# Rows of 1 / rms by a diagonal and a product with ones in place of a store and a load

## The chip, the core and the metric

The kernel runs on one core of a Trainium2 chip. The core has five engines, each with an instruction queue of its own that it works through in order: TensorE (PE in the profile; the load of its weights is shown apart as PEld), VectorE (DVE), ScalarE (ACT), GpSimd (POOL) and SyncE (SP), which in this kernel issues nearly all of the DMAs. Engines meet by semaphores. TensorE reads its operands from SBUF and writes to PSUM, which is cut into banks of 128 partitions by 512 float32 numbers. SBUF and PSUM have 128 partitions; an engine that works by elements works within each partition, so a value that lies along the partitions has to be moved before it can be used along the free axis.

The metric is the device time of one execution, in microseconds (us); lower is better.

## The reference, cut to what matters

One layer of an encoder, on x of 2048 tokens by 1024 channels in float32, with a memory of 256 tokens:

```python
xn = rmsnorm(h, norm_mix_g)
proj = xn @ w_in                      # columns: q, k, v (512 each), u, y (512 each)
q, k = rope(q, positions), rope(k, positions)
attn = dilated_mixture_attention(q, k, v)      # 8 heads of 64, three windows
uc = centred_depthwise_conv(u, conv_w, conv_b)
rec = bidirectional_rglru(uc, ...) * gelu(y)   # gates, two scans over the tokens
h = h + concatenate([attn, rec]) @ w_out
h = h + memory_cross_attention(rmsnorm(h, norm_cross_g), rmsnorm(mem, norm_mem_g),
                               w_cq, w_ck, w_cv, w_co)   # 4 heads of 128
hid = square(relu(rmsnorm(h, norm_mlp_g) @ w_mlp_in))    # 4096 channels
h = h + hid @ w_mlp_out
return rmsnorm(h, norm_final_g)

def rmsnorm(x, g):
    return x * rsqrt(mean(x * x, axis=-1) + 1e-6) * g
```

So there are five norms: of x, of the memory, and of h three times. Each needs one number 1 / rms for every token.

## The kernel before, in words

**Layout.** Activations are kept with channels on the partitions and tokens on the free axis: a tile is 128 channels by 512 tokens. A norm sums over channels, so over the partitions, and its factor 1 / rms differs from token to token, so along the free axis. To multiply a tile by it, the factors of 512 tokens have to lie in every one of the 128 partitions: a **row** tile of 128 x 512, all partitions alike. Since the factor of a token can be taken out of a product over channels, the products run on the values without the norm, and the row is multiplied onto the result as it leaves PSUM. The gain g goes into the operands.

**Products in three parts.** Every large product is `mm3` (L120 to L123): both operands are split into a high and a low part in float32r, and three matmuls (high by high, high by low, low by high) add up in one PSUM bank. That is why L121, L122 and L123 come three at a time in the profile. PSUM banks are given out by tag: `ps("mm")` takes turns between m0 and m1, `ps("mmb")` between m0, m1 and b; each tag has two banks in the phases that matter here (b has two, a has two). Most instructions have tile names, which the profile shows: `xh`, `xl` are the parts of x, `wh`, `wl` those of weights, `mh`, `ml` of the memory.

**How a row is made (`RowSum`, L125 to L173).** `add` squares a tile on ACT (L142) and adds it to `ss` on POOL or DVE (L144). `columns` (L147 to L156) sums `ss` over the partitions: for each 128 tokens one matmul of `ss` by a column of ones (L151), into a bank of tag a, so that the sums of 128 tokens lie along the partitions, one column for each 128. DVE copies these columns out (L155), and POOL makes 1 / rms of them in two instructions (`rstd_of`, L116 to L118). From the columns the row is then made in one of two ways:

- `rows` (L158 to L161): SP stores the columns to a line in DRAM, 4 bytes apiece (L160), and loads the line back into all 128 partitions (L161). SP issues the load only after the store has landed.
- `rows_now` (L163 to L173): DVE multiplies the identity by the columns into `dg`, four diagonal 128 x 128 blocks beside each other (L167); PE multiplies a 128 x 128 tile of ones by it in float32, which puts into every partition the one entry of each column (L172), in a bank of tag b; ACT copies the bank into the row (L173). The tile of ones is allocated and set by POOL each time (L171).

**Where rows are made.** Fifteen rows go by `rows`, five by `rows_now`:

- *The memory*, one row `rbm` of 256 tokens, in `memory_kv` (L294), after the first of eight column blocks of the keys and values; L296 multiplies it onto `em`.
- *x*, four rows `rbn` of 512 tokens, two for each half B of the tokens, in `row_tables` (L349 to L353), called by `uy_unit` after the second product of the first unit in each 512 tokens; L416 multiplies them onto `e`, and `fill_tables` multiplies them into the tables of rope. Only the columns of all 16 blocks of 128 tokens stay (`rsb`). The first half of the tokens comes round once more later (for v, k and q), and `tables` loads its row again from the same line (L344).
- *v*, two rows `svr` of 256 numbers, in `v_unit` (L455). They do not come from activations but from the columns of the v weights: 1 / rms of each column, used to bring v to a size that fits float16 (L458), and taken out again later by `dsc`.
- *h after the first residual*, four rows `rb1`, in `half_out` (L911 to L955): the sums of block b are made while block b + 1 runs, `columns` ahead of its tile 4 and `rows` ahead of its tile 5; those of the last block stand behind its last tile. Used in `query` (L1003 to L1014).
- *h after the second residual*, four rows `rb2`, in the loop of the cross attention (L1235 and L1246) and, the last, at the start of the MLP (L1391). Used by `t_raws` (L1099 on).
- *h after the third residual*, five rows by `rows_now` in `close` (L1425): they are the last thing before the output is written, 512 or 256 tokens each.

**What sets the order.** The code is written in Tile, a framework that allocates tiles, sets the semaphores and plans the order of each engine's queue from priorities (mostly the order of the code) and its own estimates of durations; the order that comes out can differ from that of the text. In the first stage, `block` (L582 on) runs over units of the combined projection: u and y of the first half of the tokens, the memory, u and y of the second half, then v, k and q of both halves. From the second half on, the steps of the RG-LRU (`lru`, L470 on: convolution, gates, scans) are a generator that `pace` advances by 1.3 steps for each part of a unit, so that DVE, ACT and POOL do the RG-LRU while PE does the projection. The convolution loads `u` back from DRAM (L492); its gates take banks of tag a (L518 on) and two small `mm3` each.

Then the attention of the eight heads, the output projection (`half_out`), the cross attention with the output of block b - 1 woven into block b, and the MLP in two large stages.

**Names that the change touches**, beside those above: the DRAM lines `rs_d`, `rsm_d`, `sv_d`, `r1_d`, `r2_d` (L60 to L64); `small` (constants); `vs`, the `RowSum` for v (L595), whose tiles are taken from the rings `rl` and `rh` of the rope; the `RowSum` of `Cross.co` (L1067), whose tiles for the fourth block lie in other pools; and `ss` and `sq`, the tiles of a `RowSum`.

## Time and profile before

| | |
|---|---|
| time, median of 3 runs | 2923.38 us (2919.47 to 2930.01) |
| the profiled execution's own time | 2928.47 us |
| its span, first instruction to last | 2926.6 us |
| mean granted TensorE clock | 0.942 |
| rows that go by store and load | 15 |
| rows that go by diagonal and product | 5 |

The page gives the span in 40 equal slices; with 2926.6 us a slice is 73.2 us. Each digit is the busy share in tenths, PEclk the granted TensorE clock in tenths of full speed, DMA the mean busy share of the core's 16 DMA engines.

```profile
PE   7897776776779989897997899989999999999997
DVE  6644656765678878634567754474447999999997
ACT  5527355461646656623444233343333333334342
POOL 2222120203334434343124655555655776666652
PEclk9998888888789999898998999999999999999999
DMA  7452334426667876554344433343336222122213
```

Slices 1 to 10 are the combined projection with the RG-LRU beside it, 11 to 16 the attention, 17 and 18 the output projection, 19 to 22 the cross attention, and from there on the MLP with the final norm. In the queues of DMA nearly all of the packets belong to SP's issues (q1); POOL issues a few itself (q0).

```profile
q1 hardware_dynamic: 262864, 342.19, 38.3%
q0 software_dynamic: 4288, 27.27, 4.0%
```

Columns: packets, MB, share of the 16 engines' span. In the rows of groups, an instruction stands with its line, engine, operation, output and input tiles, count, then busy time in all and mean ns of one, then the idle time of that engine just before them and what ended most of it. In the rows of a timeline, the first number is the start in us from the start of the span, the second the duration, and the bracket holds the idle time before and the instruction that ended it.

### The profile page before, as it was taken

The numbers are of one execution on the slowest core, as the hardware profiler recorded it, in microseconds if no ns is written. First come the engines' busy times: TensorE is split into PE (matmuls) and PEld (weight loads), VectorE is DVE, ScalarE is ACT, GpSimd is POOL, SyncE is SP. The second block draws the span as 40 slices with busy tenths as digits, with TensorE's granted clock in tenths as the row PEclk, the third lists the DMA queues.
The fourth block names the chain that finished last, engine by engine and source line by source line (L and its number), as shares of the span: only waits on it lengthen the run. The fifth ranks groups of instructions, "written<-read, shape, count | busy, mean of one in ns | idle before, by whom it ended". The sixth has DMA issues, their size and how long they took to land. (4 is left out here: it accounts for less than half of the span.)

```text
span 2926.6 us, 39992 instructions
## 1 busy us (share of the span) xinstructions
PE 2590.2 (89%) x14074; PEld 2196.7 (75%) x14074; DVE 2010.9 (69%) x3361; ACT 1277.1 (44%) x2349; POOL 1256.2 (43%) x888
## 2 busy tenths in 40 slices
PE   7897776776779989897997899989999999999997
PEld 6776665665679989786885788868887777778776
DVE  6644656765678878634567754474447999999997
ACT  5527355461646656623444233343333333334342
POOL 2222120203334434343124655555655776666652
PEclk9998888888789999898998999999999999999999
DMA  7452334426667876554344433343336222122213
GB/s 194 144 133 82 105 81 145 123 96 156 180 170 189 216 181 155 187 160 123 101 136 142 143 109 112 109 140 112 112 108 216 86 73 87 65 87 80 72 58 115
DMA packets 267352, 372.00 MB, mean 127 GB/s; under 512 B 93072, under 2 KB 139792, under 8 KB 264080
## 3 DMA queue, kind: packets, MB, share of 16 engines
q1 hardware_dynamic: 262864, 342.19, 38.3%
q0 software_dynamic: 4288, 27.27, 4.0%
q8 instruction: 111, 1.82, 0.3%
q14 instruction: 89, 0.73, 0.1%
HBM read 254.73 MB, written 114.65 MB: 126 GB/s over the span
## 5 line engine op out<-in xcount | busy, mean ns | idle before, releaser
L1304 ACT ACTIVATE c<-raw 128x512 fp32r<-128x512 f32 x162 | 102.2, 632 | 272.2 <-PE m L122 147.5
L1155 POOL TENSOR_TENSOR wl<-wr,wh 128x512 fp32r<-128x512 f32 x96 | 145.4, 1515 | 150.2 <-ACT wh L1154 150.1
L1154 ACT ACTIVATE wh<-wr 128x512 fp32r<-128x512 f32 x128 | 80.9, 632 | 287.4 <-PE m L122 153.9
L763 ACT ACTIVATE sm<-sm,obp 128x256 f32<-128x256 f32 (+1 forms) x384 | 161.9, 468 | 48.1 <-DVE obp L760 41.4
L1155 DVE TENSOR_TENSOR wl<-ws,wh 128x512 fp32r<-128x512 f32 x96 | 81.0, 843 | 130.0 <-ACT wh L1154 124.7
L235 POOL TENSOR_TENSOR wl<-wraw,wh 128x512 fp32r<-128x512 f32 x48 | 71.0, 1484 | 198.0 <-ACT wh L234 195.5
L760 DVE CUSTOM_DVE_ANT_0 sm<-a,msk 128x256 f32<-128x256 f32 (+1 forms) x384 | 131.2, 371 | 31.9 <-PE a L757 28.2
L121 PE MATMUL m<-xh,wh 128*128 128x512 f32 x328 | 132.6, 404 | 19.6 <-ACT xh L329 8.1
L775 ACT ACTIVATE ph<-b 128x512 f16<-128x512 f32 (+1 forms) x192 | 100.4, 523 | 94.1 <-PE b L772 88.6
L1176 DVE TENSOR_TENSOR c<-m,c 128x512 f32<-128x512 f32 x64 | 44.2, 690 | 139.9 <-PE m L123 137.9
L776 DVE SCALAR_TENSOR_TENSOR pl<-b,ph 128x512 f16<-128x512 f32 (+1 forms) x192 | 114.6, 598 | 26.5 <-ACT ph L775 22.7
L122 PE MATMUL m<-xl,wh 128*128 128x512 f32 x328 | 131.8, 402 | 0.3 <-DVE xl L330 0.3
L772 PE MATMUL b<-prt,sm 128*128 128x128 f32 x640 | 108.5, 285 | 26.2 <-DVE pl L776 17.2
L123 PE MATMUL m<-xh,wl 128*128 128x512 f32 x328 | 130.9, 399 | 0.0
L1305 POOL TENSOR_TENSOR wh<-raw,c 128x512 fp32r<-128x512 f32 x58 | 93.6, 1631 | 78.1 <-ACT c L1304 66.1
L702 POOL TENSOR_SCALAR kc<-kh 128x1024 fp32r<-128x1024 f32 x32 | 68.6, 2144 | 129.6 <-PE a L756 117.4
L756 PE MATMUL a<-kc,qb 128*128 128x256 f32 x256 | 108.7, 425 | 6.0 <-DVE obp L760 5.9
L1177 DVE SCALAR_TENSOR_TENSOR c<-c 128x512 f32<-128x512 f32 x96 | 111.6, 1163 | 1.0
L234 ACT ACTIVATE wh<-wraw 128x512 fp32r<-128x512 f32 x96 | 57.8, 623 | 118.2 <-DMA wraw<-in_w_in 70.0
L1154 ACT ACTIVATE wh<-ws 128x512 fp32r<-128x512 f32 x96 | 60.5, 630 | 109.6 <-PE m L122 107.9
L123 PE MATMUL m<-t3h,wl 128*128 128x512 f32 x276 | 107.6, 390 | 0.4 <-POOL wl L1155 0.3
L121 PE MATMUL m<-wh,xh 128*128 128x256 f32 x192 | 62.1, 328 | 51.3 <-DVE v L458 33.9
(556 smaller groups left out, 9789.6 us busy)
## 6 DMA issues: line engine op xcount, KB each, us to landing
wr<-in_w_m SPq DMA_DIRECT2D x64, 512.0 KB
hid_d<-c SPq DMA_DIRECT2D x128, 256.0 KB
wraw<-in_w_in SPq DMA_DIRECT2D x80, 256.0 KB
raw<-in_w_m SPq DMA_DIRECT2D x33, 512.0 KB
rawt<-hid_d SPq DMA_DIRECT2D x26, 512.0 KB
t0h<-hid_d SPq DMA_DIRECT2D x26, 512.0 KB
o_d<-obp SPq DMA_DIRECT2D x16, 528.0 KB
obr<-o_d SPq DMA_DIRECT2D x16, 528.0 KB
```

The source lines that it names most:

```text
L121: pe.matmul(o, ah, bh, start=start, stop=False, **kw)
L122: pe.matmul(o, ah, bl, start=False, stop=False, **kw)
L123: pe.matmul(o, al, bh, start=False, stop=stop, **kw)
L756: pe.matmul(so, q0, kh[:, w0:w0 + 256], start=True, stop=False)
L760: dve.tensor_tensor_reduce(out=sm, in0=sps[:, 256 * z + o0:256 * z + o0 + kw], in1=msk[:, m:m + kw], op0=ALU.add, op1=ALU.min, scale=1.0, ...
L763: exps.append(act.activation(sm, sm, AF.Exp, scale=-1.0, bias=self.obp[:, oc, 65:66]))
L772: pe.transpose(pt[:, c0:c0 + 128], self.sm[:, z, 128 * g:128 * g + 128], idt)
L776: dve.scalar_tensor_tensor(self.pl[:, :w], pt[:, :w], 1024.0, self.ph[:, :w], op0=ALU.mult, op1=ALU.subtract)
L1154: act.activation(h, self.a[n], AF.Copy)
L1155: last[n % 2] = (pool if n % 2 else dve).tensor_tensor(l, self.a[n], f32(h), op=ALU.subtract).ins
L1177: dve.scalar_tensor_tensor(z, z if n < 6 else o, 0.0, z, op0=ALU.max, op1=ALU.mult)
L1304: act.activation(h[-1], tk, AF.Copy)
```

## The change

`rows` and `rows_now` become one method `rows(dst, bank="b")`, which makes the row by the diagonal and the product. All 15 rows that went by DRAM now go this way. The tile of ones is a constant `all1`, set once by POOL at the start. The rows of the memory, of x and of v take a bank of tag a, all others one of tag b. Four of the five lines in DRAM are gone; `rs_d` stays for the second pass over the first half of the tokens, and is written from one partition of the finished row, 2 KB at once, when B is 0. Tiles for `dg` come from the ring `rl` for v, from the ring of `c_` for the fourth block of the cross attention, and otherwise from a new tag `dg` in the pool of each `RowSum`. In `half_out`, `columns` stands ahead of tile 2 of the next block, and `rows` ahead of its tile 4.

```diff
@@ -58,10 +58,6 @@
         return dram.tile(shape, d, name=name)
 
     rs_d = dt_("rs_d", [S])
-    rsm_d = dt_("rsm_d", [256])
-    sv_d = [dt_(f"sv_d{i}", [256]) for i in range(2)]
-    r1_d = dt_("r1_d", [4, 512])
-    r2_d = dt_("r2_d", [4, 512])
     u_d = dt_("u_d", [4, P, S])
     gy_d = dt_("gy_d", [4, P, S])
     rec_d = dt_("rec_d", [4, P, S])
@@ -107,6 +103,8 @@
     pool.memset(nhalf, -0.5)
     ones = small("ones", [P, 1])
     pool.memset(ones, 1.0)
+    all1 = small("all1", [P, P])
+    pool.memset(all1, 1.0)
     dsc = small("dsc", [P, 4])
     hpi = small("hpi", [P, 1])
     pool.memset(hpi, TWO_PI / 4)
@@ -155,21 +153,14 @@
             dve.tensor_copy(r, o[:, 0:nt])
             rstd_of(r, r, nt)
 
-        def rows(self, dst, line):
-
-            dma(ap(line, 0, [[1, P], [P, self.n // P]]), self.r)
-            dma(dst, ap(line, 0, [[0, P], [1, self.n]]))
-
-        def rows_now(self, dst):
+        def rows(self, dst, bank="b"):
 
             nt = self.n // P
             dg = self.tile("dg", 1).rearrange("p (j n) -> p j n", n=P)
             dve.tensor_tensor(dg, idt[:, None, :].to_broadcast([P, nt, P]),
                               self.r[:, :, None].to_broadcast([P, nt, P]), op=ALU.mult)
-            o = ps("b")[:, 0:self.n]
-            one = self.pl.tile([P, P], F32, tag="one", name="one")
-            pool.memset(one, 1.0)
-            pe.matmul(o, one, dg.rearrange("p j n -> p (j n)"), start=True, stop=True)
+            o = ps(bank)[:, 0:self.n]
+            pe.matmul(o, all1, dg.rearrange("p j n -> p (j n)"), start=True, stop=True)
             act.activation(dst, o, AF.Copy)
 
     class Head:
@@ -291,7 +282,7 @@
                         k == 0, k == 7)
                 if c == 0:
                     sm.columns()
-                    sm.rows(rbm, rsm_d)
+                    sm.rows(rbm, "a")
                 e = p1.tile([P, 256], F32, tag="em", name="em", bufs=2)
                 dve.tensor_tensor(e, o[:, :256], rbm, op=ALU.mult)
                 eh = p1.tile([P, 256], F32R, tag="eh", name="eh", bufs=2)
@@ -350,7 +341,9 @@
 
             c = 8 * B + 4 * th
             s.columns(rsb[:, c:c + 4])
-            s.rows(rbn[:, 512 * th:512 * th + 512], ap(rs_d, 1024 * B + 512 * th, [[1, 512]]))
+            s.rows(rbn[:, 512 * th:512 * th + 512], "a")
+            if B == 0:
+                dma(ap(rs_d, 512 * th, [[512, 1], [1, 512]]), rbn[0:1, 512 * th:512 * th + 512])
 
         def fill_tables(B, rbn, cosT, sinT):
             c1 = 6.28125
@@ -452,7 +445,7 @@
                         if sums:
                             sc = slice(2 * n2, 2 * n2 + 2)
                             sums.columns(svc[:, sc])
-                            sums.rows(svr[n2], sv_d[n2])
+                            sums.rows(svr[n2], "a")
                             dve.reciprocal(dsc[:, sc], svc[:, sc])
                             sums = None
                         dve.scalar_tensor_tensor(v[:, 256 * z:256 * z + 256], oz, rsb[:, r:r + 1], svr[n2],
@@ -594,6 +587,7 @@
                 if kind == "v" and B == 1:
                     vs = RowSum(p2, 1, 256, rings={
                         "ss": lambda: p2.tile([P, 512], F32, tag="rl", name="vss", bufs=2),
+                        "dg": lambda: p2.tile([P, 512], F32, tag="rl", name="vdg", bufs=2),
                         "sq": lambda: p2.tile([P, 512], F32, tag="rh", name="vsq", bufs=2)})
                 W = first if n == 0 and first else unit_w(w_in[wi], sums=vs)
                 step = pace
@@ -932,10 +926,10 @@
                 ah, al = nxt
                 ss = RowSum(aw, 2)
                 for dt in range(8):
+                    if b > 0 and dt == 2:
+                        prev.columns()
                     if b > 0 and dt == 4:
-                        prev.columns()
-                    if b > 0 and dt == 5:
-                        prev.rows(rb1[b - 1], r1_d[b - 1])
+                        prev.rows(rb1[b - 1])
                     sl = slice(128 * dt, 128 * dt + 128)
                     rt = aw.tile([P, 512], F32, tag="h1", name="h1", bufs=4)
                     dma(rt, hp_d[b, dt])
@@ -952,7 +946,7 @@
                 rb1.append(rows())
                 prev = ss
             prev.columns()
-            prev.rows(rb1[3], r1_d[3])
+            prev.rows(rb1[3])
 
         rb1, rb2 = [], []
         qh_w = cqp.tile([P, 8, 512], F32R, name="cqh")
@@ -1065,7 +1059,8 @@
                 if dt == 0:
                     self.ss = RowSum(wp, eng=dve) if self.b < 3 else RowSum(kp, eng=dve, rings={
                         "ss": lambda: ip.tile([P, 512], F32, name="ss"),
-                        "sq": lambda: wp.tile([P, 512], F32, tag="sq", name="sq", bufs=2)})
+                        "sq": lambda: wp.tile([P, 512], F32, tag="sq", name="sq", bufs=2),
+                        "dg": lambda: c_.tile([P, 512])})
                 sl = slice(128 * dt, 128 * dt + 128)
                 ht = wp.tile([P, 512], F32, tag="ht", name="ht", bufs=3)
                 dma(ht, h1_d[self.b, dt])
@@ -1232,7 +1227,7 @@
             if before and b < 3:
                 before.ss.columns()
                 rb2.append(rows())
-                before.ss.rows(rb2[-1], r2_d[b - 1])
+                before.ss.rows(rb2[-1])
             if b == 3:
                 sums = before.ss
             before = C
@@ -1243,7 +1238,7 @@
             if dt == 6:
                 sums.columns()
                 rb2.append(rows())
-                sums.rows(rb2[2], r2_d[2])
+                sums.rows(rb2[2])
         ahead(100)
 
 
@@ -1388,7 +1383,7 @@
             if i == 0 and n == 2:
                 rb2.append(rows())
                 before.ss.columns()
-                before.ss.rows(rb2[3], r2_d[3])
+                before.ss.rows(rb2[3])
             if i == 15 and n > 0:
                 t_part(nT, n - 1)
             if i == 16 and n == 0:
@@ -1424,7 +1419,7 @@
 
     def close(B, ss, t0, t1):
         rb = rows()
-        return [ss.columns, lambda: ss.rows_now(rb[:, 0:t1 - t0]), lambda: finish(B, t0, t1, rb)]
+        return [ss.columns, lambda: ss.rows(rb[:, 0:t1 - t0]), lambda: finish(B, t0, t1, rb)]
 
     acc = []
     for B in range(2):
```

## The prediction

> **What bounds the kernel now.** The page comes first: it says that TensorE (PE) is the busiest engine, but that it is not busy all the time.
>
> ```profile
> span 2926.6 us, 39992 instructions
> PE 2590.2 (89%) x14074; PEld 2196.7 (75%) x14074; DVE 2010.9 (69%) x3361; ACT 1277.1 (44%) x2349; POOL 1256.2 (43%) x888
> ```
>
> PE is idle for 2926.6 - 2590.2 = 336 us, so an edit that removes waits is worth what it removes from this idle time, and PE work that it adds counts in full where PE is full. Next I read the table of who waited for whom and picked out what waits for a row (L161 is the load of a row, L160 the store before it).
>
> ```profile
> DVE e L416 <- DMA rbn<-rs_d: 28.1, 3, 14.9
> DVE v L458 <- DMA svr<-sv_d: 17.5, 2, 9.9
> ```
>
> VectorE (DVE) stands 28.1 + 17.5 us for rows. A DVE wait is only a loss if PE waits too. So I went through the timeline of PE for its longest idle stretches and looked in the timelines of DVE and SyncE at what stood just before each.
>
> ```profile
> 63.80 0.69 DVE L416 TENSOR_TENSOR e<-m,rbn 128x512 f32<-128x512 f32 x1 [11.28 <-DMA rbn<-rs_d]
> 64.63 0.77 PE L121 MATMUL m<-xh,wh 128*128 128x512 f32 x1 [6.28 <-DVE e L416]
> ...
> 128.50 0.33 SPq L161 DMA_DIRECT2D rbm<-rsm_d  x1
> 128.93 1.47 SPq L233 DMA_DIRECT2D wraw<-in_w_cv  x3
> 133.55 0.76 DVE L296 TENSOR_TENSOR em<-m,rbm 128x256 f32<-128x256 f32 x2 [3.51 <-DMA rbm<-rsm_d]
> 134.12 0.55 PE L121 MATMUL m<-mh,wh 128*128 128x256 f32 x1 [8.41 <-DVE em L296]
> ...
> 195.86 0.33 SPq L161 DMA_DIRECT2D rbn<-rs_d  x1
> 196.28 0.38 SPq L492 DMA_DIRECT2D u<-u_d  x1
> 201.69 0.77 PE L121 MATMUL m<-xh,wh 128*128 128x512 f32 x1 [5.25 <-ACT uh L500]
> ...
> 268.26 0.37 SPq L160 DMA_DIRECT2D sv_d<-svc  x1
> 278.23 0.32 SPq L161 DMA_DIRECT2D svr<-sv_d  x1
> 281.32 0.48 DVE L458 SCALAR_TENSOR_TENSOR v<-m,rsb,svr 128x256 f32<-128x256 f32 x1 [9.86 <-DMA svr<-sv_d]
> 281.86 0.58 PE L121 MATMUL m<-wh,xh 128*128 128x256 f32 x1 [9.17 <-DVE v L458]
> ...
> 413.24 0.58 PE L121 MATMUL m<-wh,xh 128*128 128x256 f32 x1 [7.01 <-DVE v L458]
> ```
>
> Five of PE's idle stretches end with a row: 6.28, 8.41, 9.17 and 7.01 us directly (PE has filled its PSUM banks, and the DVE instruction that empties one waits for the row), and 5.25 us indirectly (the load of u stands on SyncE behind the load of a row). Sum 36.1 us. A row takes long because it goes out and back: in the fourth place 278.23 - 268.26 = 10.0 us pass between the issue of the store and that of the load, and 3.1 more until v starts. SyncE stands meanwhile, and loads queue behind L161: in the second place the three of wraw, issued from 128.93.
>
> The view by windows then shows a second price: the clock that PE is granted after each of these.
>
> ```profile
> 64.63:70.00 5.37, 5.37 (x13) 4.21 (x14) 3.24 (x6) 2.78 (x6) 0.00 (x0) 0.50 0.78 264
> 134.12:140.00 5.88, 5.72 (x29) 5.52 (x29) 5.42 (x9) 3.02 (x7) 2.65 (x2) 0.61 0.60 190
> 201.70:207.00 5.30, 5.30 (x13) 4.20 (x14) 5.30 (x9) 1.17 (x2) 0.26 (x1) 0.51 0.52 169
> 281.86:286.40 4.54, 4.54 (x25) 4.54 (x26) 3.22 (x5) 0.00 (x0) 0.00 (x0) 0.61 0.05 13
> 413.24:418.50 5.26, 5.26 (x24) 5.26 (x25) 2.56 (x4) 0.00 (x0) 0.44 (x1) 0.50 0.20 53
> 1306.00:1312.00 6.00, 6.00 (x28) 4.97 (x27) 1.38 (x2) 1.26 (x2) 3.98 (x4) 1.00 0.61 181
> 1324.35:1331.00 6.65, 6.65 (x22) 5.68 (x23) 0.16 (x1) 0.00 (x0) 2.80 (x5) 0.58 1.05 240
> ```
>
> Columns: stretch, length, busy time and count of PE, PEld, DVE, ACT, POOL, then clock, DMA share, GB/s. Undisturbed the clock is 1.00 (the window from 1306), after a gap 0.50 to 0.61. The length times what is missing from 1 is lost: 2.7, 2.3, 2.6, 1.8 and 2.6 us, in all 12.0.
>
> **The change, part by part.** *Removed: the store and the load of 15 rows* (1 of memory, 4 of x, 2 of v, 4 of r1, 4 of r2). The first two gaps lie ahead of the RG-LRU work and have full queues behind them; I count them whole: 6.28 + 2.7 + 8.41 + 2.3 = 19.7 us. The three others lie where the RG-LRU steps run beside.
>
> ```profile
> 262.00:400.00 138.00, 101.48 (x533) 88.25 (x533) 77.51 (x105) 66.95 (x101) 25.96 (x30) 0.84 0.34 97
> 480.00:640.00 160.00, 113.88 (x549) 95.05 (x549) 110.85 (x151) 90.92 (x129) 24.13 (x20) 0.83 0.38 118
> ```
>
> In the second of these stretches no row is made, yet PE is as little busy (71%) as in the first (74%): something else limits there too, and takes over part of a freed wait. Bounds: nothing to all. I take half: (5.25 + 2.6 + 9.17 + 1.8 + 7.01 + 2.6) / 2 = 14.2 us.
>
> In the output projection (half_out) a sixth gap may shrink.
>
> ```profile
> 1310.30 6.83 SPq L941 DMA_DIRECT2D h<-hp_d  x2
> 1317.70 0.38 SPq L161 DMA_DIRECT2D rb<-r_d  x1
> 1321.13 1.26 POOL L144 TENSOR_TENSOR ss<-ss,sq 128x512 f32<-128x512 f32 x1 [8.81 <-ACT sq L142]
> 1324.35 0.58 PE L151 MATMUL a<-ones,ss 128*128 128x1 f32 x2 [8.99 <-POOL ss L144]
> ```
>
> The last column sums wait 8.99 us because the last tiles of the residual arrive late; 6.65 x 0.42 = 2.8 us of slow clock follow. The late load (in the two issues from 1310.30) stands ahead of L161, so this row does not hold it; the three rows before it have pushed the loads back and took DMA time. Between 0 and 11.8 I take half, 5.9 us. For r1 and r2 otherwise nothing waits for the row, so their removed loads gain nothing more. Removed waits: 19.7 + 14.2 + 5.9 = 39.8 us.
>
> *Added: 15 diagonals (DVE), 15 float32 products (PE), 15 copies (ACT).* The kernel has five such rows already, at its end, so they have prices here.
>
> ```profile
> L172 PE MATMUL b<-t1h,one 128*128 128x512 f32 x4 | 2.1, 618 | 1.3 <-DVE t1h L167 1.3
> L172 PE MATMUL b<-t0l,one 128*128 128x512 f32 x2 | 1.1, 644 | 0.0
> 2908.53 0.59 PE L172 MATMUL b<-t0l,one 128*128 128x256 f32 x2
> L167 DVE TENSOR_TENSOR t1h<-prt,rr 128x512 f32<-128x512 f32 x2 | 1.4, 684 | 0.1
> ```
>
> A row of 512 takes PE 3.2 / 3 = 1.07 us (two instructions), one of 256 takes 0.59: 12 x 1.07 + 3 x 0.59 = 14.6 us of PE, counted in full, since once the gaps are gone PE is what is left. DVE (684 ns a row) and ACT (busy 44% of the span) work beside PE; only at the start of the MLP is DVE itself full.
>
> ```profile
> 1587.00:1650.00 63.00, 42.33 (x151) 32.63 (x152) 57.19 (x65) 24.51 (x45) 42.96 (x22) 0.79 0.41 131
> ```
>
> DVE is busy 57.2 of 63 us there: the two diagonals of the last r2 rows count, 2 x 0.68 = 1.4 us.
>
> *Added waits.* PE takes its queue in order, so a product that comes to its turn before its diagonal stops every matmul behind it, and DVE, ACT and the stores behind those. Of the five rows of before, four had work queued behind them, and these stood 1.3 us in all (group above), 0.33 each: 15 x 0.33 = 4.9 us. Lower bound 0; the upper bound is the whole path from the column sums to the product.
>
> ```profile
> 2915.87 0.16 DVE L155 COPY rr<-a 128x2 f32<-128x2 f32 x1 [1.37 <-PE a L153]
> 2917.61 1.22 PE L172 MATMUL b<-t0l,one 128*128 128x256 f32 x2 [1.78 <-DVE t0l L167]
> ```
>
> That is 1.37 + 2917.61 - 2915.87 = 3.1 us with empty queues, where nothing is left to do beside it: 15 x 3.1 = 47 us. I keep 4.9, the nearer case, with matmuls queued.
>
> *Moved: the column sums of r1 from tile 4 to tile 2 of the next block* (and the row from 5 to 4), so 24 matmuls earlier, about 5.1 us (28 in 6.00 us in the window from 1306).
>
> ```profile
> 1294.96 2.66 POOL L144 TENSOR_TENSOR ss<-ss,sq 128x512 f32<-128x512 f32 x2 [8.94 <-ACT sq L142]
> 1301.10 0.61 PE L151 MATMUL a<-ones,ss 128*128 128x1 f32 x5
> ```
>
> For the third block the sums end at 1297.6, and PE would ask at 1301.1 - 5.1 = 1296.0: a new wait of 1.6 us, less if the loads come earlier. From 0 to 1.6 I take 1.0. *The ones tile*: four of the five memsets of the closing rows had waited on POOL for the product before, with nothing due there; worth nothing. The new store of the first two x rows (2 KB each) is only read again when the first half comes round for v, k and q; nothing.
>
> **The sum.** -39.8 + 14.6 + 1.4 + 4.9 + 1.0 = -17.9 us. The profiled execution took 2928.5 us; it lies 5.1 above the median of the three runs, 2923.4. Taken from the median: 2905.5 us, -0.6%.
>
> *A rule weighed.* The Trainium skill (TensorE: Matmul & The Clock Gate, Part 1: The HAM clock gate) says that an idle window of about 3.4 us drops the array to half clock, and that about 3.4 us of work bring it back; that would be an estimated 1.7 us for each gap. The windows above agree on the half clock (0.50) and show a longer recovery, 1.8 to 2.8 us. By the page the sum would be some 3 us smaller, 2908.6.
>
> **The rivals.** *Everything goes.* All six gaps and their slow clock vanish: 36.1 + 12.0 + 11.8 = 59.9 us; against 20.9 of cost (14.6 + 1.4 + 4.9) that is -39.0, so 2884. For it: behind SyncE's waits stand loads (the three wraw loads right after 128.50), and in the third stretch without a row PE may be limited by things that rows had delayed. Against: the 71% above. Chance 0.22.
>
> *The next wait takes over.* Only the two early gaps go, 19.7 us, and 20.9 are paid and the 1.0 of the moved sums: +2.2, so 2926. For it: the RG-LRU stretches without rows idle as much. Against: in the fourth gap DVE did nothing else for 9.86 us, and the convolution stood behind v in its queue. Chance 0.16.
>
> *PE stands for the chain.* In blocks 0 and 1 and in half_out the product comes up in PE's queue before the path through DVE, POOL and DVE is done. With gains of 39.8 and other costs of 17.0 (14.6 + 1.4 + 1.0) the edit turns slower from a mean stand of (39.8 - 17.0) / 15 = 1.5 us per row; at 3.1 us it gives -39.8 + 17.0 + 47 = +24, so 2948. For it: the path is 3.1 us and PE has no second queue. Against: of the four rows with work behind them three stood for nothing. Chance 0.12.
>
> **How the numbers follow.** The forecast has 0.50, for 2895 to 2914 (from somewhat over a quarter to three quarters of the terms that I halved); everything goes 0.22 (2877 to 2895); the next wait 0.16 (2915 to 2932); PE stands 0.12 (above 2932). A measurement of this kernel can tell about 0.3%, 8.8 us, from no change. Faster by more than that, below 2914.6: 0.50 + 0.22 = 0.72; within it 0.16; slower 0.12. The range that holds 8 in 10 reaches from the low end of everything-goes to the high end of the next wait, with the ends cut a little: 2878 to 2931.
>
> **What would show it.** Right: no instruction waits for rbn, rbm or svr by DMA; PE's gaps before e, em and v are gone, and the windows behind them show a clock near 1.00; the 15 products show 1.07 and 0.59 us with PE idle under 0.4 us before most. Wrong: PE idle of 1.5 us or more before most of the products (third rival); a gap of the old length at the old place, ended by another load, by ACT tr or by a PSUM bank of tag a, which the x, memory and v rows now share with the RG-LRU gates (second rival); or a gap at another place of the same stretch, since the order of the instructions is planned anew. The sum itself falls if the 8.99 us before the last column sums stay, or if the slow clock comes back at places where it was 1.00.

## The result, and where the time went

| | before | after |
|---|---|---|
| median of the runs | 2923.89 us (2919.47 to 2930.01, 4 runs) | 2870.6 us (2869.74 to 2880.11, 4 runs) |
| ratio | | 0.9834, 95% interval 0.9811 to 0.9857 |
| span of the profiled execution | 2926.6 us | 2868.9 us |
| mean granted clock | 0.942 | 0.952 |

The changed kernel is 53.3 us faster, three times the 17.9 us that were forecast, and outside the range. In two of the later batches it ran again beside the kernel before: 2876.7 against 2914.5 us and 2879.4 against 2942.0, so 37.8 and 62.6 us. Over all batches it is mostly the kernel before that differs, from 2914.5 to 2944.7 us. The page of the changed kernel begins so:

```profile
span 2868.9 us, 40008 instructions
PE 2585.6 (90%) x14104; PEld 2186.2 (76%) x14104; DVE 2027.9 (71%) x3376; ACT 1285.1 (45%) x2366; POOL 1256.8 (44%) x884
```

PE is idle for 2868.9 - 2585.6 = 283 us, against 336 before, and it is busy 4.6 us less, although 15 products were added, since the mean granted clock is higher.

To find the stages in which the time went, four tiles serve as marks: `sm` (attention), `qf` (cross attention), `c<-m,c` (first half of the MLP) and `rr` (last column sums of the final norm). The view of one tile gives, behind "min/median/max", the start of the first and of the last instruction. Before:

```profile
L760 DVE CUSTOM_DVE_ANT_0 sm<-a,msk x384: 273/411/426, 751.2 to 1194.0; 128x256 f32<-128x256 f32 x128, 128x128 f32<-128x128 f32 x64
L1011 DVE TENSOR_TENSOR qf<-m,rb x16: 669/692/692, 1331.3 to 1527.7; 128x512 f32<-128x512 f32 x16
L1176 DVE TENSOR_TENSOR c<-m,c x64: 676/691/692, 1617.6 to 2243.6; 128x512 f32<-128x512 f32 x64
L155 DVE COPY rr<-a x14: 144/160/164, 119.7 to 2915.9; 128x4 f32<-128x4 f32 x11, 128x2 f32<-128x2 f32 x3
```

And after:

```profile
L754 DVE CUSTOM_DVE_ANT_0 sm<-a,msk x384: 272/412/427, 703.2 to 1135.5; 128x256 f32<-128x256 f32 x128, 128x128 f32<-128x128 f32 x64
L1005 DVE TENSOR_TENSOR qf<-m,rb x16: 682/691/693, 1267.1 to 1459.5; 128x512 f32<-128x512 f32 x16
L1171 DVE TENSOR_TENSOR c<-m,c x64: 676/692/693, 1552.6 to 2177.9; 128x512 f32<-128x512 f32 x64
L153 DVE COPY rr<-a x14: 144/160/164, 114.9 to 2857.3; 128x4 f32<-128x4 f32 x11, 128x2 f32<-128x2 f32 x3
```

| stage | before | after | difference |
|---|---|---|---|
| projection with RG-LRU, to the first `sm` | 751.2 | 703.2 | -48.0 |
| attention, first to last `sm` | 442.8 | 432.3 | -10.5 |
| output projection, to the first `qf` | 137.3 | 131.6 | -5.7 |
| cross attention, to the first `c` | 286.3 | 285.5 | -0.8 |
| MLP, first half, to the last `c<-m,c` | 626.0 | 625.3 | -0.7 |
| MLP, second half, to the last `rr` | 672.3 | 679.4 | +7.1 |

The projection has nearly all of it. The 10.5 us of the attention I put down to chance: its instructions have not changed, and in the 18 executions of the experiments this stretch took 424.8 to 445.9 us. The second half of the MLP gives 7 us back.

What the prediction wanted to see at the new rows, in the timeline of PE after:

```profile
30.80 1.12 PE L163 MATMUL a<-dg,all 128*128 128x512 f32 x2 [2.03 <-DVE dg L160]
116.59 1.22 PE L163 MATMUL a<-dg,all 128*128 128x256 f32 x2 [5.07 <-DVE dg L160]
172.35 2.05 PE L163 MATMUL a<-dg,all 128*128 128x512 f32 x2 [2.92 <-DVE dg L160]
```

and in the groups by shape, with the busy time, the mean ns and the idle time before:

```profile
L163 PE MATMUL b<-dg,all 128*128 128x512 f32 x14 | 7.4, 609 | 1.7 <-DVE dg L160 1.7
L163 PE MATMUL a<-dg,all 128*128 128x512 f32 x8 | 5.4, 762 | 7.2 <-DVE dg L160 7.2
L163 PE MATMUL b<-c,all 128*128 128x512 f32 x2 | 2.0, 1126 | 1.8 <-DVE c L160 1.8
L163 PE MATMUL a<-vdg,all 128*128 128x256 f32 x4 | 1.4, 424 | 1.1 <-DVE dsc L449 0.8 <-DVE vdg L160 0.3
L163 PE MATMUL a<-dg,all 128*128 128x256 f32 x2 | 1.2, 716 | 5.1 <-DVE dg L160 5.1
```

No instruction waits for `rbn`, `rbm` or `svr` by DMA any more, and the gaps before `e`, `em`, `uh` and the first `v` of both rows are gone or down to 1.5 us. One sign against the forecast is there too, a longer gap at another place of the same stretch: PE's wait for weights just ahead of the second `v` row was 9.32 us (ended at 394.60) and is 13.10 (ended at 356.88). The 15 products take 17.4 us of PE, and PE stands 16.9 us before them, where 4.9 were allowed. So the costs were larger than forecast, 34 us and not 21, and the gains were larger still. Where did they come from?

### The profile page after: what moved, and what is told of

Its sections match the earlier page's. It is cut to its first block, busy times and chain, and to the rows that moved or that the text cites. A ratio compares the mean times of both kernels' runs of the same rounds, so it can differ in the third digit from the quotient of the medians.

```text
span 2868.9 us, 40008 instructions
## 1 busy us (share of the span) xinstructions
PE 2585.6 (90%) x14104; PEld 2186.2 (76%) x14104; DVE 2027.9 (71%) x3376; ACT 1285.1 (45%) x2366; POOL 1256.8 (44%) x884
## 5 line engine op out<-in xcount | busy, mean ns | idle before, releaser
L766 PE MATMUL b<-prt,sm 128*128 128x128 f32 x640 | 107.8, 283 | 17.3 <-DVE pl L770 9.3
L750 PE MATMUL a<-kc,qb 128*128 128x256 f32 x256 | 108.5, 425 | 5.9 <-DVE obp L754 5.9
L1300 POOL TENSOR_TENSOR wl<-raw,c 128x512 fp32r<-128x512 f32 x58 | 93.3, 1625 | 19.8 <-ACT c L1299 19.8
L751 PE MATMUL a<-kc,qb 128*128 128x256 f32 x256 | 101.6, 397 | 0.0
```

Of the source, the lines that this page charges most:

```text
L750: pe.matmul(so, q0, kh[:, w0:w0 + 256], start=True, stop=False)
L766: pe.transpose(pt[:, c0:c0 + 128], self.sm[:, z, 128 * g:128 * g + 128], idt)
L1300: self.eng[n].tensor_tensor(l[-1], tk, f32(h[-1]), op=ALU.subtract)
```

## The experiments

In every batch the kernel before ran beside the others on the same chip. The kernel before took 2944.7, 2914.5, 2936.3, 2941.1 and 2942.0 us in the five batches, so times are compared within a batch, or by the start of the attention in the trace. Without an edit the changed kernel and those with its instructions in the projection start the attention at 703.2 to 711.4 us.

**The seven rows of the projection by DRAM again.**

```diff
-            s.rows(rbn[:, 512 * th:512 * th + 512], "a")
+            s.rows(rbn[:, 512 * th:512 * th + 512], "a", ap(rs_d, 1024 * B + 512 * th, [[1, 512]]))
...
-                    sm.rows(rbm, "a")
+                    sm.rows(rbm, "a", rsm_d)
...
-                            sums.rows(svr[n2], "a")
+                            sums.rows(svr[n2], "a", sv_d[n2])
```

> The changed kernel with the seven rows of the projection (memory 1, x 4, v 2) made by store and load again; r1 and r2 stay on chip. In the two traces the changed kernel is 48.1 us ahead when the attention starts. If that comes from these seven rows, this kernel takes 2871 + 48 - 12 (products 6.7 us and stands of a few us that go) to 2871 + 48, so 2907 to 2919 us, and the gaps before e, em and v are back. If the lead came from the new order of the instructions and not from the rows, under 2890 us.

Measured: 2932.2 us (before 2944.7; ratio 0.9963, 0.9941 to 0.9985).

```profile
L760 DVE CUSTOM_DVE_ANT_0 sm<-a,msk x384: 271/412/426, 764.0 to 1196.3; 128x256 f32<-128x256 f32 x128, 128x128 f32<-128x128 f32 x64
```

The attention starts 61 us later than in the changed kernel, and the time lies above the 2907 to 2919 us that were expected: more is lost than expected. The gain lies in these seven rows.

**Store and load for nobody**, to part the wait of SyncE from the wait for the row. The rows are made on chip; SyncE stores and loads beside.

```diff
+            if line is not None:
+                dma(ap(line, 0, [[1, P], [P, self.n // P]]), self.r)
+                dma(dead[:, 0:min(self.n, 480)], ap(line, 0, [[0, P], [1, min(self.n, 480)]]))
             nt = self.n // P
```

> The changed kernel, which in addition stores the columns of the seven rows of the projection in 4-byte pieces and loads the line back into a tile that nobody reads (480 columns instead of 512 for x). The rows themselves come from the product, so no engine waits for them; SyncE stands between store and load as before. Theory S (what was lost was SyncE's queue: loads and stores behind the row's load come late): 2890 us or more, with gaps before uh, v and wh that the changed kernel lacks. Theory W (what was lost was the wait of VectorE for the row itself): within 5 us of 2871. Theory D (4-byte packets slow the DMA engines): as much slower as the kernel with the dead stores alone.

**The store alone**, without the load line of the last diff.

> The changed kernel with the same seven stores of columns in 4-byte pieces, and no load. SyncE does not stand, nobody waits. Theory D: 2880 us or more. Theories S and W: 2867 to 2876 us.

Measured on the same chip: with both 2917.9 us (ratio 0.9911, 0.9883 to 0.9939), with the store alone 2901.5 us (0.9854, 0.9824 to 0.9884). In this order, the start of the attention:

```profile
L763 DVE CUSTOM_DVE_ANT_0 sm<-a,msk x384: 273/413/427, 748.0 to 1183.9; 128x256 f32<-128x256 f32 x128, 128x128 f32<-128x128 f32 x64
```

```profile
L761 DVE CUSTOM_DVE_ANT_0 sm<-a,msk x384: 273/412/426, 732.4 to 1166.6; 128x256 f32<-128x256 f32 x128, 128x128 f32<-128x128 f32 x64
```

Seven stores of 1 to 2 KB, for which nobody waits, cost 29 us (732.4 - 703.2). SyncE's stand adds 16, the wait for the row (764.0) another 16. This was in none of the terms of the prediction. What happens is in the view by windows; the store is issued at 29.1 us, and the columns after the length are busy time of PE, PEld, DVE, ACT and POOL, clock, DMA share and GB/s:

```profile
34.00:38.00 4.00, 4.00 (x23) 3.48 (x22) 1.87 (x4) 0.26 (x1) 0.00 (x0) 1.00 0.57 24
```

In the changed kernel, without the store:

```profile
34.00:38.00 4.00, 4.00 (x16) 3.24 (x15) 4.00 (x5) 3.29 (x8) 1.67 (x1) 0.80 0.62 200
```

The DMA engines are as busy as without the store (0.57 and 0.62), and move an eighth. ACT and POOL run dry, because the weights that they split are late.

**The stores in other pieces.** The order of the instructions of all engines is the same in these four and in the 4-byte store; only the access pattern of the dead store differs. In the order of the added lines: 128 pieces of 16 or 8 bytes side by side; one piece; 128 pieces of 4 bytes side by side; the same 512 bytes apart.

```diff
-                dma(ap(line, 0, [[1, P], [P, self.n // P]]), self.r)
+                dma(ap(line, 0, [[self.n // P, P], [1, self.n // P]]), self.r)
+                dma(ap(line, 0, [[self.n // P, 1], [1, self.n // P]]), self.r[0:1])
+                dma(ap(line, 0, [[1, P], [1, 1]]), self.r[:, 0:1])
+                dma(ap(wide_d, 0, [[128, P], [1, 1]]), self.r[:, 0:1])
```

> The kernel with the seven dead stores, but each partition writes its columns side by side: 128 packets of 16 bytes (8 for the memory and v) a store instead of 512 (256) of 4 bytes, 896 packets in all instead of 2816. The order of all engines' instructions is the same as with the 4-byte stores, which took 2901.5 us, 31 more than the changed kernel. Theory N (each small packet costs a fixed time): 31 x 896 / 2816 = 10 us, so 2881 us. Theory F (a store in small pieces stops the DMA for a fixed time, whatever its count): 2896 to 2905 us. Theory 4 (only pieces as small as 4 bytes do): 2868 to 2875 us.

> The same again with one packet a store: only the first partition writes its columns (16 or 8 bytes). The order of all instructions is the same as with the 4-byte stores. If the small packets cost the time (theories N, F by count of packets, 4): 2867 to 2874 us. If the 31 us came from the new order of the instructions that the additional stores brought: 2895 us or more.

> The same order of instructions; each store writes only the first column, 128 packets of 4 bytes, the same count of packets as the stores of 16-byte pieces that cost nothing. Theory size (a 4-byte piece costs whatever the count): a quarter to all of what the stores of 512 such packets cost, 8 to 30 us, so 2878 to 2900 us. Theory count (the many packets are what costs): 2867 to 2873 us.

> The kernel with seven dead stores of 128 packets of 4 bytes, with the pieces 512 bytes apart instead of side by side. Same order of instructions. Side by side they brought the start of the attention from 706.5 (one packet a store) to 721.2 us. If it is the size of the piece: 717 to 725 us. If it is pieces of 4 bytes that fall beside each other: 703 to 709 us.

The 4-byte stores ran once more beside the third:

> The kernel with seven dead stores of 4-byte pieces once more, on the chip of this batch: its first run was on another chip than those with 16-byte pieces and with one packet (2869 us both). If the 4-byte pieces stop the DMA on every chip: 2885 to 2905 us, and the attention starts at 725 us or later (732.4 in the first run, 703.2 in the changed kernel). If only that chip did: under 2878 us.

| dead store, seven times | time, us | ratio to before, 95% interval | start of attention |
|---|---|---|---|
| 512 (256) pieces of 4 bytes, again | 2897.5 | 0.9873 (0.9847 to 0.9899) | 731.8 |
| 128 pieces of 4 bytes, side by side | 2897.6 | 0.9875 (0.9851 to 0.9898) | 721.2 |
| 128 pieces of 4 bytes, 512 bytes apart | 2879.3 | 0.979 (0.9769 to 0.9812) | 708.5 |
| 128 pieces of 16 or 8 bytes, side by side | 2868.7 | 0.9823 (0.9784 to 0.9862) | 703.5 |
| one piece | 2868.8 | 0.983 (0.9793 to 0.9867) | 706.5 |

So it is neither the order of the instructions (one piece costs nothing) nor the count of packets (128 of 16 bytes cost nothing), nor the size of a piece alone (4 bytes, 512 bytes apart: 708.5). It is pieces of 4 bytes that lie side by side in DRAM. On the chip of the first two lines of the table, two kernels without such stores in the projection (r1 or r2 by DRAM, below) start the attention at 705.2 and 707.6 us, so it is not the chip either. With 128 instead of 512 pieces the projection loses little more than half as much (721.2). The times of the two do not show this; in the profiled executions the attention took 443.6 and 437.0 us, which takes back 6.6 of the 10.6 us.

The window of above with pieces of 16 bytes, where the DMA engines are busier still and move 272 GB/s:

```profile
34.00:38.00 4.00, 4.00 (x23) 3.47 (x22) 4.00 (x6) 3.58 (x8) 1.64 (x1) 1.00 0.91 272
```

**The kernel before, with nothing but larger pieces.** This is the test of the kernel before itself, all 15 rows, same order of instructions. The store now lays the tokens into the line in another order, and the load takes them as they lie: this kernel leaves out the right order of the tokens in its rows, and serves to measure the time.

```diff
-            dma(ap(line, 0, [[1, P], [P, self.n // P]]), self.r)
+            dma(ap(line, 0, [[self.n // P, P], [1, self.n // P]]), self.r)
```

> The kernel before, with nothing changed but the pieces of its 15 stores: each partition writes its columns side by side, 16 or 8 bytes instead of 4. The rows are loaded as before, so they have the tokens in another order (that part of the computation is changed); the order of all engines' instructions is that of the kernel before. SyncE stands and VectorE waits as before. Theory D (of the 48 us by which the projection became shorter, about 26 are the 4-byte pieces, as the dead stores cost them when added to the changed kernel, 706 to 732 us at the start of the attention): the attention starts at 722 to 730 us instead of 751 to 764, and the time is 25 to 40 us under that of the kernel before on the same chip. Theory SW (the dead stores only showed a cost that the kernel before hides in its waits): attention at 742 us or later, under 12 us gained.

Measured: 2858.6 us, against 2941.1 before on the same chip: ratio 0.9718 (0.9692 to 0.9743), 82 us, where at most 25 to 40 were expected. The changed kernel with one diagonal built elsewhere (below) took 2871.4 us in the same batch, so larger pieces alone bring no less than the whole change. The start of the attention and the waits of SyncE for the store of a row (us in total, times, longest):

```profile
L760 DVE CUSTOM_DVE_ANT_0 sm<-a,msk x384: 274/414/426, 710.9 to 1142.5; 128x256 f32<-128x256 f32 x128, 128x128 f32<-128x128 f32 x64
```

```profile
SPq L161 <- DMA r_d<-rr: 8.1, 4, 5.2
SPq L161 <- DMA sv_d<-svc: 5.7, 2, 2.9
SPq L161 <- DMA rsm_d<-rr: 2.2, 1, 2.2
SPq L161 <- DMA rs_d<-rsb: 1.3, 1, 1.3
```

The same view of the kernel before:

```profile
SPq L161 <- DMA r_d<-rr: 49.4, 6, 10.6
SPq L161 <- DMA rs_d<-rsb: 29.9, 4, 8.0
SPq L161 <- DMA sv_d<-svc: 18.1, 2, 9.5
SPq L161 <- DMA rsm_d<-rr: 6.0, 1, 6.0
```

103.4 us of waiting become 17.3. For the first row of x, store (L160) to load (L161), the timeline of SyncE before:

```profile
29.91 0.38 SPq L160 DMA_DIRECT2D rs_d<-rsb  x1
...
39.26 0.33 SPq L161 DMA_DIRECT2D rbn<-rs_d  x1
```

and with larger pieces:

```profile
28.95 0.33 SPq L160 DMA_DIRECT2D rs_d<-rsb  x1
...
31.04 0.38 SPq L161 DMA_DIRECT2D rbn<-rs_d  x1
```

9.4 us from store to load become 2.1. For the second row, stored at 47.90 us in the kernel before and loaded from 58.92, it looks like this between the two:

```profile
50.00:54.00 4.00, 4.00 (x19) 3.30 (x18) 2.52 (x5) 0.00 (x0) 1.17 (x2) 1.00 0.93 85
54.00:58.00 4.00, 4.00 (x20) 3.27 (x18) 0.00 (x0) 0.00 (x0) 0.00 (x0) 1.00 0.90 24
```

From 54 us on the DMA engines are 90% busy and move 24 GB/s, and DVE, ACT and POOL have nothing to do. A row by store and load is cheap; the pieces of the store were dear.

**r1 and r2 by DRAM again**, the rest as changed:

```diff
-                        prev.rows(rb1[b - 1])
+                        prev.rows(rb1[b - 1], line=r1_d[b - 1])
...
-                before.ss.rows(rb2[-1])
+                before.ss.rows(rb2[-1], line=r2_d[b - 1])
```

> The changed kernel with the four rows r1 of the output projection by store and load again, their columns ahead of tile 4 and the rows ahead of tile 5. From the traces: between the last tile of the attention and the first use of r1 the changed kernel gains 5.7 us, in which four products of 1.07 us are already paid. If the 8.99 us before the last column sums come back with their slow clock: 2871 + 6 = 2877 us (2874 to 2882). If the products cost what the row did: 2868 to 2872 us.

> The changed kernel with the four rows r2 by store and load again. Nobody waited for them in the kernel before; here four products (4.3 us) and PE's stands before them (0.74, 0.73, 0.25 and 1.82 us) go. If that is all: 2871 - 8 = 2863 us. If the 4-byte stores slow the loads of the cross attention by as much: 2868 to 2874 us; if by more (as in the projection, some 4 us a store): 2879 us.

Measured on one chip (before 2936.3): r1 by DRAM 2890.1 us (ratio 0.9857, 0.9828 to 0.9886), more than the 2874 to 2882 expected; r2 by DRAM 2869.4 us (0.9777, 0.9743 to 0.981). With r1 by DRAM the wait of the last column sums is back:

```profile
1266.48 1.87 PE L153 MATMUL a<-ones,ss 128*128 128x1 f32 x8 [11.18 <-POOL ss L146]
```

In the kernel before with larger pieces it is not there, and no `h` waits for its load, whereas before 12 of them waited 38.9 us. So that wait too was the stores of 4 bytes. For r2 the row on chip is no gain: nobody waited for it, and the products cost. The time alone does not tell r2 by DRAM from the changed kernel, but the trace does: from the first `qf` to the first `c` it takes 277.4 us (277.7 in the next kernel with r2 by DRAM, below), where the 15 traced executions with r2 on chip take 283.6 to 292.6.

**The price of a product.** All 20 products done twice:

```diff
-            pe.matmul(o, all1, dg.rearrange("p j n -> p (j n)"), start=True, stop=True)
+            for _ in range(2):
+                pe.matmul(o, all1, dg.rearrange("p j n -> p (j n)"), start=True, stop=True)
```

> The changed kernel with each of the 20 products of ones done twice. The 15 new rows cost PE 14.6 us more by the durations in the prediction (1.07 and 0.59 us), the five old ones 4.4 us. If PE is what is left everywhere: 2871 + 19 = 2890 us. If PE's time in the projection is hidden by the waits of the RG-LRU (6.1 us of the 14.6): 2884 us. If hardly any of it is on the path: under 2878 us.

> The changed kernel once more, beside the kernel before on the chip of this batch, since the chip of the batch before this one ran the kernel before in 2945 us, not in 2924. If what the change removes is what differs between chips, it takes 2865 to 2878 us here too, whatever the kernel before takes; if the whole chip is slower, some 0.7% more, about 2890 us.

Measured on one chip: 2885.8 us against 2876.7 of the changed kernel (2871.6 to 2883.9); the spans of the profiled executions are 2884.7 and 2869.8. So 9 to 15 us of the 19, though the intervals of the two ratios overlap (0.9855 to 0.9936 and 0.9817 to 0.9911): a product's time seems to be on the path for about half or more.

**Earlier column sums for x and the memory**, so that PE does not stand before the product:

```diff
                     mm3(o[:, :256], ...)
+                    if c == 0 and k == 0:
+                        sm.columns()
                 if c == 0:
-                    sm.columns()
                     sm.rows(rbm, "a")
...
-            s.columns(rsb[:, c:c + 4])
...
                         if c == 0:
+                            r = 8 * B + 4 * th
+                            sums[th].columns(rsb[:, r:r + 4])
                             continue
```

> The changed kernel with the column sums of the memory and of x issued earlier: after the first of the 24 matmuls of the first memory block, and after the first instead of the second product of a unit of x, so that the chain through VectorE, GpSimd and VectorE runs beside a product. In the changed kernel PE stands 2.03, 1.41, 5.07, 0.87 and 2.92 us before these five products, in all 12.3 us, with about 2 us of slow clock after the longer ones. If PE's stands are what is lost: 2852 to 2862 us. If the waits move to another place: 2867 to 2874 us.

Measured: 2870.5 us. The edit took away only part of what it was made for: before the products of the memory and of x PE still stands 8.7 of the 12.3 us (4.97 for the memory, 5.07 without the edit). The last `e` comes 6.6 us earlier than in the changed kernel (237.7 and 244.3 us), the attention starts at 703.5 instead of 703.2. The waits of PE for the gates of the RG-LRU are no longer (for `tr` 37.0 and 36.8 us in all). At 594 us 2.1 us of the lead are left, and more than that goes in the wait before the first product of the attention, here and in the changed kernel:

```profile
691.37 0.58 PE L752 MATMUL a<-kh,qb 128*128 128x256 f32 x1 [32.22 <-DVE t L378]
691.03 0.58 PE L750 MATMUL a<-kh,qb 128*128 128x256 f32 x1 [28.38 <-DVE t L378]
```

DVE makes these `t` of the rope late because it waits for a store of `rl` to `k_d` to land first (the longest such wait is 17.9 us here and 15.3 in the changed kernel). So the next waits take the gain back, as the second rival had it, but not those of the gates.

**Where the MLP lost 7 us.** The last r2 row takes its diagonal from the ring `c_`, of which the MLP's tiles then each get the next place. Here it is built in the row's own tile:

```diff
-            dg = self.tile("dg", 1).rearrange("p (j n) -> p j n", n=P)
+            dg = (dst if here else self.tile("dg", 1)).rearrange("p (j n) -> p j n", n=P)
...
-                before.ss.rows(rb2[3])
+                before.ss.rows(rb2[3], here=True)
```

> The changed kernel, with the diagonal of the last r2 row built in the row's own tile instead of a tile from the ring of c_. From the first hidden tile to the last column sums of the final norm the changed kernel takes 1304.7 us (2857.3 - 1552.6) and 1303.2 in its second run, the kernel before 1298.3, the one with r2 by DRAM 1295.2. If the tile taken from the ring shifts the places of all later tiles of the MLP, this stretch falls to 1294 to 1299 us, and the time by 5 to 9 us. If the MLP lost these microseconds in another way (the products of r2 lie ahead of this stretch): 1302 to 1306 us.

```profile
L1170 DVE TENSOR_TENSOR c<-m,c x64: 677/692/692, 1559.2 to 2182.3; 128x512 f32<-128x512 f32 x64
L153 DVE COPY rr<-a x14: 145/162/163, 114.5 to 2855.8; 128x4 f32<-128x4 f32 x11, 128x2 f32<-128x2 f32 x3
```

The second half of the MLP takes 2855.8 - 2182.3 = 673.5 us, near the 672.3 of before, and the stretch from the first `c`, expected at 1294 to 1299 us, 1296.6. In the 14 traced executions with a tile from the ring the second half takes 675.3 to 680.2 us, in the six without 670.7 to 673.5. So the tile from the ring was the cause, for some 6 of the 7 us. The time was 2871.4 us (ratio 0.9769, 0.9745 to 0.9794) and does not show the gain; in the profiled execution the projection ran longer (711.4 us to the attention).

**Two attempts at something better.** First the changed kernel with r2 by DRAM and the earlier column sums:

> The changed kernel with the four rows r2 by store and load, as nobody waits for them, and the early columns of the memory and of x. r2 by DRAM took 2857.0 us of span against 2869 of the changed kernel; the early columns alone brought nothing at the end (703.5 against 703.2 us at the start of the attention). So 2853 to 2862 us; if r2 by DRAM had a lucky run, 2866 to 2872 us.

Measured: 2859.5 us (2852.1 to 2868.3), ratio 0.9727 (0.9695 to 0.9758). Then the kernel before with 16-byte pieces and the tokens in the right order, by column sums over every fourth token; the changed kernel ran beside it:

```diff
+                parts += [self.ss.rearrange("p (q j) -> p j q", j=nt)[:, j] for j in range(nt)]
```

> The kernel before, with stores in pieces of 16 or 8 bytes and the rows right: the column sums for the row take every fourth token (every second for 256), so that partition p holds tokens 4p to 4p + 3 and the line lies in the order of the tokens. x and v keep their old columns too, 20 small matmuls more (about 2 us of PE). No product of ones, no diagonal. The kernel before with 16-byte pieces and wrong order took 2858.6 us. So 2857 to 2866 us, and under the changed kernel beside it. If taking the stationary operand from every fourth element is slow, or the second column sums stand in PE's way: 2868 us or more.

> The changed kernel beside it on the same chip: 2866 to 2878 us, as in its two runs before.

Measured: 2895.8 us (ratio 0.9832, 0.9802 to 0.9861); the changed kernel 2879.4 (0.9774, 0.9746 to 0.9802). A miss. The stores are not the reason: SyncE waits 18.5 us for them in all, against 17.3 without the right order of the tokens. Part of the reason is in its timeline of PE and its windows:

```profile
36.46 2.81 PE L154 MATMUL a<-ones,ss 128*128 128x1 f32 x16
39.13 0.78 PE L121 MATMUL b<-xh,wh 128*128 128x512 f32 x1
```

```profile
38.00:42.00 4.00, 4.00 (x13) 3.44 (x14) 3.07 (x7) 3.04 (x8) 2.35 (x2) 0.61 0.52 189
```

Twice as many sums take 2.81 us, where 8 contiguous ones take 0.95 in the changed kernel, and the clock falls to 0.61 behind them without a gap. There are four such runs of sums in the projection, and behind three of them the clock of the next 3 us is 0.50 to 0.54. An estimate from these figures (2.81 - 0.95 us for each run, and half of 3 us behind three of them) is 4 x 1.9 + 3 x 1.5 = 12 us. By as much the attention starts later than without the right order (722.8 and 710.9). Of the rest, 14 us lie in the attention (445.9 and 431.6), which has no such sums; that is open. The version with r2 by DRAM ran in another batch, in which the kernel before took nearly the same time (2941.1 and 2942.0 us): with 2859.5 us it is the fastest kernel here whose rows are in the order of the tokens, some 20 us under the changed one of that other batch, though the intervals of the two ratios overlap.

## Why the prediction was wrong

**What failed is the step "A row takes long because it goes out and back".** It took the 10 us from store to load for the way through DRAM, and so counted as removed only what waits for the row: five gaps and half of a sixth, 39.8 us. In the projection the way takes 2 to 3 us, as the kernel before with larger pieces shows. The rest was that the DMA engines move little while the 4-byte pieces are under way (24 GB/s at a share of 0.90), and this delayed other transfers too: weights, `u`, the residual. By the kernel before with larger pieces this is some 40 of the 48 us in the projection (751.2 and 710.9, on two chips), and the whole sixth gap. The rows that would have shown it were to be had: 0.90 DMA share at 24 GB/s with three idle engines.

**Halving the three late gaps** was wrong in kind: there the lengths of gaps do not add up. The last `e` is the last step ahead of that stretch (the first of the three gaps, at 201.69, lies ahead of it); before and in the changed kernel:

```profile
L416 DVE TENSOR_TENSOR e<-b,rbn x11: 676/683/693, 45.0 to 262.0; 128x512 f32<-128x512 f32 x11
```

```profile
L409 DVE TENSOR_TENSOR e<-b,rbn x11: 679/684/692, 34.5 to 244.3; 128x512 f32<-128x512 f32 x11
```

With the earlier column sums it comes at 237.7, in the kernel before with larger pieces at 230.0 us. From there to the attention the four take 489.2, 458.9, 465.8 and 480.9 us. Of the last three, whoever is early waits more later. With the earlier column sums it is the wait before the attention above; with larger pieces the lead of 14.3 us is gone at the weights of the second `v` unit (357.73 us, and 356.88 in the changed kernel), behind waits of 3.30 and 6.88 us for `v` and 11.53 for a gate of the RG-LRU. What a row frees ahead of this stretch is passed on only as far as the waits inside it allow.

**The rival "everything goes"** summed 59.9 us of gaps and slow clock and gave 2884. It had the same blind spot; no case of the prediction reached 2870.6, since none had a term for transfers that were late elsewhere.

**The two early gaps and the sixth** went. For the sixth, half had been kept for the late loads; they were late by the stores. At the early places the product's own stands took some back (5.07 us for the memory).

**Products:** 14.6 us forecast, 17.4 measured in the groups, and 9 to 15 of 19 when doubled: near in size, though not all of it is shown to count. **Stands:** 4.9 us forecast, 16.9 measured. The prediction took the price from closing rows with one thing to do; in the projection DVE splits weights and x, POOL splits weights, and the copy of the column sums waits its turn on DVE: for the memory the sums end at 110.24 us and are copied at 114.86, behind three splits and an `e`, and PE stands 5.07 us. The mean, 1.1 us a row, stayed under the 1.5 at which the third rival turned the edit slower; with only the gains that were forecast, costs of 34 us would have left about 6.

**Moved column sums of r1:** PE does not stand before them at 1241.43 in the changed kernel.

```profile
1241.43 0.95 PE L149 MATMUL a<-ones,ss 128*128 128x1 f32 x8
```

The term of 1.0 us was nothing. **The diagonal from the ring** was not in the prediction at all, and cost some 6 us, in the second half of the MLP, 650 us and more after the row.

**The rule weighed.** The Trainium skill (TensorE: Matmul & The Clock Gate, Part 1: The HAM clock gate) has the clock fall after an idle window; in the last experiment it fell behind three of four runs of 16 column sums, with PE busy in the records. The Trainium skill (DMA: Bandwidth & Descriptors, Specifications) also says that below 512 bytes the DMA engines read, modify and write. The runs agree that small pieces can cost, but do not show 512 bytes as the border: 16 and 8 bytes side by side cost nothing that the start of the attention shows (703.5 us), nor did 4 bytes apart (708.5).

## What to carry to other kernels

Before a wait for a DMA is priced, ask why that DMA is slow: put the GB/s beside the DMA share, and look for busy DMA engines that move little. A small store can cost far more than the one who waits for it shows, and changing its access pattern may be worth as much as removing it: here one line of it took 82 us off, though in a kernel that leaves out the order of the tokens in its rows. The one version with the right order took only 46 us off, against 63 by the changed kernel beside it, and its column sums are part of the reason. And a tile borrowed from a ring moves all later tiles of that ring.

## What the hardware showed that was not expected

Stores of 128 or more pieces of 4 bytes side by side in DRAM hold up the DMA engines for several us (the windows of 4 us above), and cost the projection 2 to 4 us each (15 to 29 us for seven); pieces of 8 or 16 bytes do not. Why is open. That neighbouring pieces are written into one stretch of DRAM by several engines would fit, but from which distance on they stop to cost, and whether 512 pieces of 16 bytes would, was not tried. Column sums with a stationary operand from every fourth element take 2.81 us for 16 (half of them contiguous) against 0.95 for 8 contiguous ones, and behind them the clock was 0.61 in a window of 4 us. Eight such sums without the contiguous ones, in the output projection of the same kernel, took 1.80 us, and the clock behind them stayed at 1.00.
